# Keeping short-lived sums in PSUM, so that VectorE reads one operand there and one in SBUF

## The chip, the cores and the metric

One core of a Trainium2 chip runs the whole program. The metric is the device time of one execution in microseconds (us): 2315.3 us, the median of 3 runs before the change (2315.18 to 2316.68).

## The reference, cut to what matters

Two transformer blocks stand one behind the other, on 512 tokens of width 1024, all in float32. The first is conditioned on a vector `c`; the second has two mixers and 64 experts.

```python
mod = silu(c) @ w_mod + b_mod                      # 1024 -> 9 * 1024
sh1, sc1, ga1, sh2, sc2, ga2, sh3, sc3, ga3 = split(mod, 9)
h = rms_norm(x, g_ffn1) * (1 + sc1) + sh1
x = x + 0.5 * (1 + ga1) * ((silu(h @ w1_gate) * (h @ w1_up)) @ w1_down)    # width 2816
h = rms_norm(x, g_mix) * (1 + sc2) + sh2
x = x + (1 + ga2) * hybrid_mixer(h)
h = rms_norm(x, g_ffn2) * (1 + sc3) + sh3
x = x + 0.5 * (1 + ga3) * swiglu(h, w2_gate, w2_up, w2_down)
x = second_block(x)          # two mixers, then a router and 64 experts
```

## The kernel before

The activations are held transposed: eight tiles `xT` of 128 features by 512 tokens. Each float32 matrix product is made of three products of rounded parts: a weight panel is rounded by ScalarE (`wh`) and its rest is taken by GpSimd in pieces of 256 columns (`wl`, line 131); an activation is split into a high part by ScalarE and a low part by VectorE (`split`, lines 105 and 106). There are eight banks of PSUM, 128 by 512 float32 each: two under the name `mm` and six under `at`.

A feed-forward stage (`ffn_lined`) goes through 22 pairs of weight panels (gate and up, 128 hidden features each), in groups of 6, 6, 5 and 5. A pair costs TensorE 48 matmuls of 512 columns into two banks of `at`. Then ScalarE takes silu of the gate (line 538), VectorE multiplies by up (line 539), and the product is split into `ah` and `al` for the down product. Behind each group, `down` goes through the eight `xT` tiles: three matmuls for each pair of the group into a bank of `mm`, and VectorE adds the result to `xT` (line 551). The first down product of a group reads the group's pairs in order, so it needs the last pair's `ah` and `al` only near its end.

In the first feed-forward stage a callback, `between`, stands behind the pairs 2 to 15. Each call computes one of 14 half chunks of 512 columns of `mod`: two loads of 1 MB (`wmod`, four buffers), eight VectorE operations that add up 128x512 rows times a column of `silu(c)` (`modacc`, lines 276 and 278, two buffers in SBUF), and three bfloat16 parts of the sum (`third`, lines 285 to 291) made by ScalarE and GpSimd in turn. Twelve thin matmuls with a column of ones add over the partitions (`mod_cols`).

A norm (`norm_after`, `norm_half`) goes by halves of 256 tokens. As each `xT` tile gets its last update, ScalarE squares it and VectorE adds the square to a sum (line 338). A matmul with ones adds over the partitions, ScalarE makes 1/rms in two steps (`rstd`, lines 317 and 318), and for each of the eight tiles VectorE scales `xT` by it (line 351), ScalarE rounds, and VectorE takes the rest (`hl`, line 355 or 359). The first half's scaling is interleaved with the second half's updates. There are three such norms: behind the first feed-forward stage, behind the first mixer, and behind the second feed-forward stage.

A scheduler sets the order of the instructions on each engine when the program is built; it goes by the order of the source, by a price for each instruction, and by which buffers it expects to be free. Each engine then executes its own queue strictly in that order.

Of the kernel before, what the change touches and what calls it, by code (L numbers as in the profile page):

```python
# [7 lines left out]
F32 = mybir.dt.float32  # L8
# [9 lines left out]
P = 128  # L18
S = 512
D = 1024  # L20
KD = D // P
# [9 lines left out]
def f32(ap):  # L31
    return ap.bitcast(F32)


class Net:
# [225 lines left out]
    def mod_rows(self, pool, rs, on_pe=False):  # L261

        nc = self.nc
        acc = self.sb(pool, [P, 512], F32, "modacc", 2)
        if on_pe:

            pr = self.ps("mm")
            for kh in range(2):
                for k in range(4):
                    self.mm(pr[32 * k:32 * k + 32], self.cpad[:, kh * 4 + k], rs[kh][:, k], kh == 0, kh == 1)  # L270
            nc.vector.tensor_copy(acc, pr)
        else:
            for k in range(KD):
                c, r = self.ccol[:, k:k + 1], rs[k // 4][:, k % 4]
                if k == 0:
                    nc.vector.tensor_scalar(acc, r, c, None, op0=ALU.mult)
                else:
                    nc.vector.scalar_tensor_tensor(acc, r, c, acc, op0=ALU.mult, op1=ALU.add)  # L278
        return acc

    def thirds(self, pool, x):

        nc = self.nc
        parts = [self.sb(pool, [P, 512], BF16, f"third{i}", 2) for i in range(3)]
        nc.scalar.activation(parts[0], x, AF.Copy)
        halves = slice(0, 256), slice(256, 512)
        for cs in halves:
            nc.gpsimd.tensor_sub(x[:, cs], x[:, cs], parts[0][:, cs])  # L288
        nc.scalar.activation(parts[1], x, AF.Copy)
        for cs in halves:  # L290
            nc.gpsimd.tensor_sub(parts[2][:, cs], x[:, cs], parts[1][:, cs])  # L291
        return parts

    def mod_cols(self, chunk, half, parts):
# [34 lines left out]

    HALVES = (slice(0, 256), slice(256, 512))  # L330

    def square(self, j, half, acc):

        sq = self.tmp()[:, :256]
        self.nc.scalar.activation(sq, self.xT[j][:, self.HALVES[half]], AF.Square)
        if acc is None:
            return sq
        self.nc.vector.tensor_add(acc, acc, sq)  # L338
        return acc

    def norm_half(self, half, acc, acol, bcol, off, hs, between=lambda j: None):

        nc = self.nc
        pn = self.ps("at")[:, :256]
        self.mm(pn, self.ones, acc, True, True)
        r = self.rstd(pn, D, 256)
        ts = self.HALVES[half]
        cs = slice(off + ts.start, off + ts.stop)
        for j in range(KD):
            t = self.tmp()[:, :256]  # L350
            nc.vector.scalar_tensor_tensor(t, self.xT[j][:, ts], acol[:, j:j + 1], r, op0=ALU.mult, op1=ALU.mult)  # L351
            H, L = (t_[:, cs] for t_ in hs[j])
            if bcol is None:
                nc.scalar.activation(H, t, AF.Copy)
                nc.vector.tensor_sub(L, t, f32(H))
            else:
                b = bcol[:, j:j + 1]
                nc.scalar.activation(H, t, AF.Identity, bias=b)
                nc.vector.scalar_tensor_tensor(L, t, b, f32(H), op0=ALU.add, op1=ALU.subtract)  # L359
            between(j)  # L360

    def norm_after(self, steps, ahead, acol, bcol, off=0):


        acc = [None, None]
        self.pe_order_from = len(self.traced())
        if off:

            tags = [f"hl{j}" for j in range(4)] + [f"hh{j}" for j in range(4, KD)]
            tags += [f"h{part}{j}" for j in range(KD) for part in "hl" if f"h{part}{j}" not in tags]  # L370
            made = {tag: self.hidden2(F32R, tag) for tag in tags}
            hs = [(made[f"hh{j}"], made[f"hl{j}"]) for j in range(KD)]
        else:
            hs = [tuple(self.sb(self.hp, [P, S], F32R, f"h{part}{j}") for part in "hl") for j in range(KD)]

        def run(half, todo):
            for j, update in todo:
                update()
                acc[half] = self.square(j, half, acc[half])

        run(0, steps[0])
        run(1, steps[1][:ahead])
        rest = steps[1][ahead:]
        self.norm_half(0, acc[0], acol, bcol, off, hs, lambda j: rest and run(1, [rest.pop(0)]))
        return hs, lambda: self.norm_half(1, acc[1], acol, bcol, off, hs)
# [121 lines left out]
    def ffn_lined(self, pool, i, wg, wu, wd, nxt, hs, second, between):  # L507

        nc = self.nc
        groups = ((0, 6), (6, 12), (12, 17), (17, 22))  # L510
        if i == 0:
            hs, done = self.first_norm(pool, wg, wu)
        else:
            panels = [self.wpanel(w, f) for f in range(2) for w in (wg, wu)]
            done = [self.ps("at") for _ in panels]
            for half, ts in enumerate(self.HALVES):
                for n, (p, (wh, wl)) in enumerate(zip(done, panels)):
                    if half == 0 and n == 1:
                        second()
                    for k in range(KD):  # L520
                        self.mm3(p[:, ts], wh[:, k], wl[:, k], hs[k][0][:, ts], hs[k][1][:, ts], k == 0, k == KD - 1)
            self.pe_order()
        for f0, f1 in groups:
            act = []
            nf = f1 - f0
            for f in range(f0, f1):
                ps = []
                for w in (wg, wu):
                    if done:
                        ps.append(done.pop(0))  # L530
                        continue
                    wh, wl = self.wpanel(w, f)
                    p = self.ps("at")
                    for k in range(KD):
                        self.mm3(p, wh[:, k], wl[:, k], hs[k][0][:, :S], hs[k][1][:, :S], k == 0, k == KD - 1)
                    ps.append(p)
                s = self.sb(pool, [P, S], F32, "silu", 2)
                self.mark = nc.scalar.activation(s, ps[0], AF.Silu)
                nc.vector.tensor_mul(s, ps[1], s)  # L539
                ah = self.sb(pool, [P, S], F32R, "ah", 7)  # L540
                al = self.sb(pool, [P, S], F32R, "al", 7)
                self.split(ah, al, s)
                act.append((ah, al))
                between(f)

            def down(j, w, ts):
                p = self.ps("mm")[:, ts]
                for k in range(nf):
                    self.mm3(p, w[0][:, k], w[1][:, k], act[k][0][:, ts], act[k][1][:, ts], k == 0, k == nf - 1)
                x = self.xT[j][:, ts]  # L550
                nc.vector.scalar_tensor_tensor(x, p, self.G[i][:, j:j + 1], x, op0=ALU.mult, op1=ALU.add)

            def load(j):
                return self.kpanel(wd[f0 * P:f1 * P, j * P:(j + 1) * P], nf, P)

            if f1 < NF:
                for j in range(KD):
                    down(j, load(j), slice(0, S))
        self.use_exp()

        held = {}

        def step(j, half):
            if j not in held:
                held[j] = load(j)
            down(j, held[j], self.HALVES[half])
            if not half and j < 4:
                del held[j]

        return self.norm_after([[(j, lambda j=j: step(j, 0)) for j in range(KD)],  # L570
                                [(j, lambda j=j: step(j, 1)) for j in (4, 5, 6, 7, 0, 1, 2, 3)]], 1, *nxt)
# [1548 lines left out]
```

## Time and profile before

| | |
|---|---|
| median of 3 runs | 2315.3 us |
| the profiled execution: time, span of its core | 2318.89 us, 2317.1 us |
| first feed-forward stage with its start | about 0 to 406 us |
| first mixer, second feed-forward stage | to about 753 us, to about 1090 us |
| second block's mixers, then router and experts | to about 1350 us, to the end |
| busy: PE, DVE, ACT, POOL | 91%, 35%, 26%, 34% of the span |

PE is TensorE, DVE VectorE, ACT ScalarE, POOL GpSimd. The profile is of one execution. A line such as L89 is the line of the kernel that issues an instruction; L89 is the one place for all matmuls, so these are told apart by their tiles. The durations of PE are modelled and overlap: the distance between the starts of two matmuls is the pace, 0.23 us for 512 columns in the full stretches.

### The profile page before, as it was taken

What the parts mean: (1) busy time and instruction counts of PE and PEld (TensorE: products, weight loads), DVE (VectorE), ACT (ScalarE), POOL (GpSimd) and SP (SyncE); (2) the same over time, 40 slices, a digit from 0 to 9 for tenths busy, and PEclk for the clock granted to TensorE, in tenths of its full rate; (3) what the DMA queues carried; (4) which work ended last, traced back from release to release, by engine and by line L of the source; (5) the groups of instructions that cost most, each with busy time, mean ns of one, the idle gap of its engine ahead of it and who ended that gap; (6) DMA issues with size and microseconds to landing.
All of it is one profiled execution on the core that took longest, in us unless ns stands there. A gap on an engine that the chain in (4) does not pass through costs nothing.

```text
span 2317.1 us, 29183 instructions
## 1 busy us (share of the span) xinstructions
PE 2103.3 (91%) x11561; PEld 1390.1 (60%) x11561; DVE 814.6 (35%) x1390; ACT 595.8 (26%) x1027; POOL 791.2 (34%) x1023
## 2 busy tenths in 40 slices
PE   8889999999998999999999999988888598888886
PEld 5767788887877888888887763332333243333332
DVE  6748321657578211112635552111111111111112
ACT  4323222465365322223524421000000000000002
POOL 2869655775543455555655300000000000000001
PEclk9999999999999999999999999999999799999997
DMA  9676322421211232333422199999999999999998
GB/s 328 222 245 218 101 86 86 110 75 38 73 46 47 80 102 83 107 101 87 107 69 83 58 378 415 421 421 421 421 421 420 378 421 420 420 421 420 421 421 302
DMA packets 275921, 550.10 MB, mean 237 GB/s; under 512 B 18461, under 2 KB 199862, under 8 KB 228678
## 3 DMA queue, kind: packets, MB, share of 16 engines
q1 hardware_dynamic: 272832, 547.78, 62.9%
q8 instruction: 92, 1.51, 0.3%
q10 hardware_dynamic: 2950, 0.43, 0.1%
q14 instruction: 47, 0.39, 0.0%
HBM read 546.06 MB, written 2.10 MB: 237 GB/s over the span
## 4 chain that ended last, share of the span: by engine, by line
PE 50%; DMA 36%; DVE 8%; POOL 3%; ACT 2%; issue 1%; SPq 0%; POOLq 0%; ACTq 0%; DVEq 0%
PE at L89 32%; PE mm L89 17%; DMA ew<-in_expert_w_gate 12%; DMA ew<-in_expert_w_down 12%; DMA ew<-in_expert_w_up 11%; POOL wl L131 2%; DVE modacc L278 1%; DMA wmod<-in_w_mod 1%; DVE tmp L351 1%; DVE tmp L338 1%; DVE hl L359 1%; POOL modacc L288 0%; POOL third L291 0%; DVE smax L866 0%; PE at L1351 0%
## 5 line engine op out<-in xcount | busy, mean ns | idle before, releaser
L131 POOL TENSOR_TENSOR wl<-wraw,wh 128x256 fp32r<-128x256 f32 (+1 forms) x790 | 613.4, 807 | 403.2 <-ACT wh L123 401.3
L89 PE MATMUL at<-ew,xg 128*32 128x512 f32 x2048 | 330.8, 647 | 71.4 <-DMA ew<-in_expert_w_up 44.4
L1814 POOL TENSOR_TENSOR sg<-oh,Gt 128x512 f32<-128x512 f32 x16 | 16.8, 1050 | 852.6 <-PE at L1866 565.5
L89 PE MATMUL at<-hh,wh 128*128 128x512 f32 (+3 forms) x800 | 298.7, 377 | 3.1 <-ACT hh L450 1.2
L123 ACT ACTIVATE wh<-wraw 128x1024 fp32r<-128x1024 f32 (+2 forms) x193 | 183.9, 954 | 454.0 <-PE at L89 187.0
L89 PE MATMUL at<-hl,wh 128*128 128x512 f32 (+3 forms) x800 | 296.5, 375 | 3.7 <-DVE hl L359 1.5
L89 PE MATMUL at<-hh,wl 128*128 128x512 f32 (+3 forms) x800 | 294.8, 373 | 0.0
L89 PEld LDWEIGHTS at<-ew,xg 128*32 128x32 f32 x2048 | 75.4, 116 | 283.9 <-issue 142.0
L89 PE MATMUL at<-ew,ehT 128*32 128x512 f32 (+1 forms) x1040 | 186.5, 599 | 18.9 <-ACT ehT L1878 10.4
L89 PE MATMUL mm<-ah,wh 128*128 128x512 f32 (+1 forms) x432 | 155.8, 361 | 22.5 <-ACT ah L105 12.8
L89 PEld LDWEIGHTS at<-hh,wh 128*128 128x128 f32 (+1 forms) x800 | 150.4, 188 | 33.3 <-ACT hh L450 3.5
L89 PEld LDWEIGHTS at<-hl,wh 128*128 128x128 f32 (+1 forms) x800 | 150.7, 188 | 32.3 <-DVE hl L359 2.4
L89 PEld LDWEIGHTS at<-oh,xn 128*128 128x128 f32 x1024 | 123.2, 197 | 73.1 <-issue 70.8
L89 PEld LDWEIGHTS at<-hh,wl 128*128 128x128 f32 (+1 forms) x800 | 150.7, 189 | 26.2
L89 PE MATMUL mm<-al,wh 128*128 128x512 f32 (+1 forms) x432 | 154.1, 357 | 2.9 <-DVE al L106 2.9
L89 PE MATMUL at<-oh,xn 128*128 128x128 f32 x1024 | 135.2, 287 | 20.8 <-DMA ew<-in_expert_w_gate 19.5
L89 PE MATMUL mm<-ah,wl 128*128 128x512 f32 (+1 forms) x432 | 153.5, 355 | 0.0
L1901 DVE TENSOR_TENSOR ewa<-ewa,mm 128x512 f32<-128x512 f32 (+1 forms) x124 | 82.9, 670 | 167.8 <-PE mm L89 167.8
L539 DVE TENSOR_TENSOR silu<-at,silu 128x512 f32<-128x512 f32 x44 | 30.3, 689 | 286.8 <-PE at L89 279.0
L1873 DVE SCALAR_TENSOR_TENSOR eh<-at,rslot,eh 128x512 f32<-128x512 f32 x16 | 17.3, 1084 | 323.4 <-PE at L89 323.4
L89 PE MATMUL mm<-ey,sgT 128*128 128x512 f32 (+1 forms) x264 | 125.0, 604 | 2.0 <-DVE ewa L1904 0.8
L89 PEld LDWEIGHTS at<-ew,ehT 128*32 128x32 f32 x1040 | 46.6, 111 | 126.4 <-issue 81.4
(483 smaller groups left out, 3118.8 us busy)
## 6 DMA issues: line engine op xcount, KB each, us to landing
ew<-in_expert_w_gate SPq DMA_DIRECT2D x128, 1024.0 KB, 19.8
ew<-in_expert_w_up SPq DMA_DIRECT2D x128, 1024.0 KB, 19.8
ew<-in_expert_w_down SPq DMA_DIRECT2D x122, 1024.0 KB, 19.8
wmod<-in_w_mod SPq DMA_DIRECT2D x36, 1024.0 KB, 8.4
wraw<-in_w_gate SPq DMA_DIRECT2D x44, 512.0 KB, 3.9
wraw<-in_w_up SPq DMA_DIRECT2D x44, 512.0 KB, 3.8
wraw<-in_w_in SPq DMA_DIRECT2D x39, 512.0 KB, 3.9
wraw<-in_w_down SPq DMA_DIRECT2D x40, 320.0 KB, 3.2
```

The source lines that it names most:

```text
L89: self.nc.tensor.matmul(out, lhsT, rhs, start=start, stop=stop, skip_group_check=open_)
L123: self.nc.scalar.activation(h[:, :cols], r[:, :cols], AF.Copy)
L131: (eng or self.nc.gpsimd).tensor_sub(l[:, cs], r[:, cs], f32(h[:, cs]))
L278: nc.vector.scalar_tensor_tensor(acc, r, c, acc, op0=ALU.mult, op1=ALU.add)
L338: self.nc.vector.tensor_add(acc, acc, sq)
L351: nc.vector.scalar_tensor_tensor(t, self.xT[j][:, ts], acol[:, j:j + 1], r, op0=ALU.mult, op1=ALU.mult)
L359: nc.vector.scalar_tensor_tensor(L, t, b, f32(H), op0=ALU.add, op1=ALU.subtract)
L539: nc.vector.tensor_mul(s, ps[1], s)
L1814: nc.gpsimd.tensor_tensor(sg.rearrange("p t (e s) -> p t e s", s=self.CAP), ov, self.G[:, :, es_].unsqueeze(3).to_broadcast(shp), op=ALU.mult)
L1873: nc.vector.scalar_tensor_tensor(hf, pu, rs, hf, op0=ALU.mult, op1=ALU.mult)
L1901: nc.vector.tensor_add(self.acc[t][:, cs], self.acc[t][:, cs], pc[:, :w])
```

## The change

Four kinds of values that lay in SBUF now lie in PSUM, in banks of `at`:

- The modulation's sum (`modacc`), from its first operation to the second subtraction. [...]
- The product of silu and up: VectorE writes it over up. `split` then reads it from there, and the bank is held until `al` is made.
- The sums of squares: the second addition writes into a bank, the later ones add there, and the last writes to SBUF again, since TensorE reads it.
- 1/rms: ScalarE writes it over the sum that it comes from.

```diff
     def mod_rows(self, pool, rs, on_pe=False):
-        acc = self.sb(pool, [P, 512], F32, "modacc", 2)
         if on_pe:
+            acc = self.sb(pool, [P, 512], F32, "modacc", 2)
...
         else:
+            acc = self.ps("at")
             for k in range(KD):
...
         nc.scalar.activation(parts[0], x, AF.Copy)
-        halves = slice(0, 256), slice(256, 512)
-        for cs in halves:
-            nc.gpsimd.tensor_sub(x[:, cs], x[:, cs], parts[0][:, cs])
+        nc.vector.tensor_sub(x, x, parts[0])
         nc.scalar.activation(parts[1], x, AF.Copy)
-        for cs in halves:
-            nc.gpsimd.tensor_sub(parts[2][:, cs], x[:, cs], parts[1][:, cs])
+        nc.vector.tensor_sub(parts[2], x, parts[1])
         return parts
...
-    def square(self, j, half, acc):
+    def square(self, n, j, half, acc):
         sq = self.tmp()[:, :256]
         self.nc.scalar.activation(sq, self.xT[j][:, self.HALVES[half]], AF.Square)
-        if acc is None:
+        if n == 0:
             return sq
-        self.nc.vector.tensor_add(acc, acc, sq)
-        return acc
+        to = self.ps("at")[:, :256] if n == 1 else acc if n < KD - 1 else self.tmp()[:, :256]
+        self.nc.vector.tensor_add(to, acc, sq)
+        return to
...
         pn = self.ps("at")[:, :256]
         self.mm(pn, self.ones, acc, True, True)
-        r = self.rstd(pn, D, 256)
+        r = self.rstd(pn, D, 256, r=pn)
...
                 self.mark = nc.scalar.activation(s, ps[0], AF.Silu)
-                nc.vector.tensor_mul(s, ps[1], s)
+                nc.vector.tensor_mul(ps[1], ps[1], s)
+                s = ps[1]
                 ah = self.sb(pool, [P, S], F32R, "ah", 7)
                 al = self.sb(pool, [P, S], F32R, "al", 7)
                 self.split(ah, al, s)
```

The scheduler orders the program anew. VectorE at the end of the first group of the first feed-forward stage, before: `silu_974` is the product of pair 5, the last of the group, `al_978` its low part, and `modacc_1432` the modulation's sum of pair 7.

```order
L276 TENSOR_SCALAR modacc_1432<-wmod_1428,ccol_153 128x512
L278 SCALAR_TENSOR_TENSOR modacc_1432<-wmod_1428,ccol_153,modacc_1432 128x512 x3
L278 SCALAR_TENSOR_TENSOR modacc_1432<-wmod_1430,ccol_153,modacc_1432 128x512 x3
L539 TENSOR_TENSOR silu_974<-at_949,silu_974 128x512
L304 TENSOR_TENSOR mod_61<-mm_1003,cols_68 128x4
L278 SCALAR_TENSOR_TENSOR modacc_1432<-wmod_1430,ccol_153,modacc_1432 128x512
L106 TENSOR_TENSOR al_978<-silu_974,ah_977 128x512
L309 SCALAR_TENSOR_TENSOR A_3_63<-mod_61,cols_68 128x4
```

The same place now: `at_943` is up and then the product of pair 5, and `at_979` the modulation's sum of pair 5 itself.

```order
L278 TENSOR_SCALAR at_979<-wmod_975,ccol_153 128x512
L280 SCALAR_TENSOR_TENSOR at_979<-wmod_975,ccol_153,at_979 128x512 x3
L280 SCALAR_TENSOR_TENSOR at_979<-wmod_977,ccol_153,at_979 128x512 x3
L541 TENSOR_TENSOR at_943<-at_943,silu_968 128x512
L280 SCALAR_TENSOR_TENSOR at_979<-wmod_977,ccol_153,at_979 128x512
L106 TENSOR_TENSOR al_972<-at_943,ah_971 128x512
L288 TENSOR_TENSOR at_979<-at_979,third_208_988 128x512
L290 TENSOR_TENSOR third_210_990<-at_979,third_209_989 128x512
L303 TENSOR_TENSOR mod_61<-mm_995,cols_68 128x4
L308 SCALAR_TENSOR_TENSOR A_3_63<-mod_61,cols_68 128x4
```

Before, the sums ran up to two pairs ahead of the pair whose product is made between them. Now each pair's product and sum stand together, and the sum of the next pair begins only behind the small operations that close this one (lines 303 and 308).

TensorE at the border of the pairs 2 and 3, before: the last matmuls of pair 2 (`at_613`), then the thin matmuls of its half chunk (`third_154` to `third_156`), twelve in one piece, and behind them pair 3.

```order
L89 MATMUL at_613<-hl_131_492,wh_606 128x512
L89 MATMUL at_613<-hh_130_490,wl_608 128x512
L89 LDWEIGHTS third_154_658
L89 MATMUL mm_667<-onesb_139,third_154_658 128x1
L89 LDWEIGHTS third_155_659
L89 MATMUL mm_667<-onesb_139,third_155_659 128x1
L89 LDWEIGHTS third_156_660
L89 MATMUL mm_667<-onesb_139,third_156_660 128x1
```

The same thin matmuls now, within pair 3's gate (`at_689`).

```order
L89 MATMUL at_689<-hh_98_337,wh_682 128x512
L89 LDWEIGHTS third_154_658
L89 MATMUL mm_665<-onesb_139,third_154_658 128x1
L89 MATMUL at_689<-hl_99_339,wh_682 128x512
L89 MATMUL at_689<-hh_98_337,wl_684 128x512
L89 MATMUL at_689<-hh_124_478,wh_682 128x512
L89 MATMUL at_689<-hl_125_480,wh_682 128x512
L89 MATMUL at_689<-hh_124_478,wl_684 128x512
L89 MATMUL at_689<-hh_126_482,wh_682 128x512
L89 LDWEIGHTS third_155_659
L89 MATMUL mm_665<-onesb_139,third_155_659 128x1
```

The first thin matmul moved behind 10 matmuls of the next gate, the second behind 16, and the remaining ten behind 20.

## Rows read from the trace of the kernel before

**Rows 1.** The page, the chain that ended last, shares of the span by engine.

```profile
PE 50%; DMA 36%; DVE 8%; POOL 3%; ACT 2%; issue 1%; SPq 0%; POOLq 0%; ACTq 0%; DVEq 0%
```

**Rows 2.** PE in order of time: start, us, instruction, [idle before <- releaser].

```profile
103.77 0.45 PE L89 MATMUL mm<-onesb,third 128*128 128x1 bf16 x12
107.90 0.50 PE L89 MATMUL mm<-ah,wh 128*128 128x512 f32 x1 [3.68 <-DVE mod L304]
119.53 0.80 PE L89 MATMUL mm<-ah,wh 128*128 128x512 f32 x1 [6.32 <-ACT ah L105]
```

**Rows 3.** DVE in order of time, the same stretch.

```profile
103.49 0.98 DVE L276 TENSOR_SCALAR modacc<-wmod,ccol 128x512 f32<-128x512 f32 x1 [6.18 <-POOL wl L131]
...
118.14 0.68 DVE L539 TENSOR_TENSOR silu<-at,silu 128x512 f32<-128x512 f32 x1
```

**Rows 4.** A stretch: length, busy PE, PEld, DVE, ACT, POOL, PEclk, DMA share, GB/s.

```profile
120.00:125.00 5.00, 4.22 (x10) 3.12 (x10) 1.66 (x2) 1.99 (x3) 4.26 (x7) 0.50 0.82 272
```

**Rows 5.** The chain in order of time, 140 to 350 us: start, us, what.

```profile
156.28 10.88 PE at L89 x48
...
266.02 10.88 PE at L89 x48
276.90 0.29 PE mm L89 x12
277.20 11.02 PE at L89 x48
...
322.16 27.26 PE mm L89 x120
```

**Rows 6.** PE in order of time, the second group's down product.

```profile
223.89 0.47 PE L89 MATMUL mm<-ah,wh 128*128 128x512 f32 x1
...
234.05 0.80 PE L89 MATMUL mm<-ah,wh 128*128 128x512 f32 x1 [6.48 <-ACT ah L105]
```

**Rows 7.** DVE groups by shape, whole span: count | busy us, mean ns | idle before.

```profile
L278 DVE SCALAR_TENSOR_TENSOR modacc<-wmod,ccol,modacc 128x512 f32<-128x512 f32 x98 | 100.2, 1023 | 3.0
...
L551 DVE SCALAR_TENSOR_TENSOR xT<-mm,G,xT 128x512 f32<-128x512 f32 x48 | 36.0, 750 | 116.3 <-PE mm L89 116.3
L539 DVE TENSOR_TENSOR silu<-at,silu 128x512 f32<-128x512 f32 x44 | 30.3, 689 | 286.8 <-PE at L89 279.0 <-ACT silu L538 7.8
```

**Rows 8.** DVE groups, 49 to 53.5 us (POOL idle), then 187 to 208 us.

```profile
L278 DVE SCALAR_TENSOR_TENSOR modacc<-wmod,ccol,modacc 128x512 f32<-128x512 f32 x6 | 4.5, 752 | 0.2
...
L278 DVE SCALAR_TENSOR_TENSOR modacc<-wmod,ccol,modacc 128x512 f32<-128x512 f32 x14 | 15.5, 1109 | 0.5
```

**Rows 9.** POOL groups, 145 to 160 us, then 187 to 208 us.

```profile
L131 POOL TENSOR_TENSOR wl<-wraw,wh 128x256 fp32r<-128x256 f32 x16 | 11.3, 738 | 5.6 <-ACT wh L123 5.6
...
L131 POOL TENSOR_TENSOR wl<-wraw,wh 128x256 fp32r<-128x256 f32 x16 | 17.0, 1095 | 0.0
```

**Rows 10.** ACT groups by shape, whole span.

```profile
L285 ACT ACTIVATE third<-modacc 128x512 bf16<-128x512 f32 x14 | 8.7, 621 | 19.3 <-DVE modacc L278 19.3
```

**Rows 11.** Stretches of the three norms.

```profile
425.00:460.00 35.00, 30.84 (x230) 29.30 (x230) 29.42 (x50) 17.34 (x36) 29.70 (x40) 0.95 0.45 121
735.00:760.00 25.00, 19.86 (x127) 17.85 (x127) 20.77 (x38) 13.62 (x28) 13.42 (x16) 0.86 0.29 85
1110.00:1130.00 20.00, 15.82 (x110) 14.33 (x108) 17.60 (x32) 9.57 (x18) 19.08 (x31) 0.91 0.67 175
```

**Rows 12.** DVE in order of time, one tile's turn in the first norm.

```profile
432.07 1.00 DVE L351 SCALAR_TENSOR_TENSOR tmp<-xT,A,tmp 128x256 f32<-128x256 f32 x1
432.99 0.96 DVE L338 TENSOR_TENSOR tmp<-tmp,tmp 128x256 f32<-128x256 f32 x1
433.87 0.47 DVE L551 SCALAR_TENSOR_TENSOR xT<-mm,G,xT 128x256 f32<-128x256 f32 x1
434.27 0.56 DVE L359 SCALAR_TENSOR_TENSOR hl<-tmp,mod,hh 128x256 fp32r<-128x256 f32 x1
```

**Rows 13.** The chain in order of time, where the norm begins.

```profile
406.52 14.90 PE mm L89 x122
```

More of the change, by code (lines that the diff above doesn't have):

```diff
@@ L362, in norm_after @@
     def norm_after(self, steps, ahead, acol, bcol, off=0):
-        acc = [None, None]
+        acc, n = [None, None], [0, 0]
         self.pe_order_from = len(self.traced())
@@ L378, in run @@
                 update()
-                acc[half] = self.square(j, half, acc[half])
+                acc[half] = self.square(n[half], j, half, acc[half])
+                n[half] += 1
         run(0, steps[0])
```

## The prediction

> **What bounds the kernel now.** I read the chain that ended last first. PE holds half of it and DMA 36% [rows 1]; the DMA share is the experts' weights in the last 970 us, which the change does not touch. So the question is where TensorE waits before that, and for whom. I then read the stretches one after the other for PE's idle time and its granted clock, and PE in order of time where it was idle. Two places stand out: the ends of the first two groups of the first feed-forward stage, and the three norms.
>
> First group: PE ends pair 5 with the thin matmuls at 103.77 + 0.45, about 104.1, and starts the down product at 107.90, after 3.68 us of waiting; it waits 6.32 us more before 119.53 [rows 2]. The second wait is for `ah` of the last pair, whose product VectorE made only at 118.14, 14 us after PE had finished the pair [rows 3]. VectorE was late because the modulation's operations stand ahead of the product in its queue, and at 103.49 it had itself waited 6.18 us for GpSimd to free a `modacc` buffer [rows 3]. [...] Second group: PE starts the down product at 223.89 and waits 6.48 us before 234.05, again for `ah` [rows 6].
>
> What these two cost, waits and slow clock together: the third group's down product, undisturbed, takes 27.26 us for 120 matmuls, 0.227 us each [rows 5], so 144 take 32.7 us. The first took from 104.1 to 156.28, 52.2 us: 19.5 lost. The second took from 223.89 to 266.02, 42.1 us: 9.4 lost [rows 2, 5, 6]. Together 28.9 us.
>
> Why VectorE and GpSimd are slow there: an addition to `modacc`, two operands from SBUF, takes 752 ns while GpSimd is idle and 1109 ns while it works; GpSimd's `wl` takes 738 ns where VectorE is nearly idle and 1095 ns beside those additions [rows 8, 9]. The update of `xT`, the same operation with one operand from PSUM, takes 750 ns in the mean of 48 [rows 7].
>
> **The change part by part.** *The modulation.* 98 additions at 1023 ns [rows 7] become additions with one operand in PSUM. No row shows VectorE writing PSUM. Bounds: 750 ns, the row that reads PSUM and has the same three inputs [rows 7], and 1109 ns, the worst of today [rows 8]; a gain below 0.75 is bounded by the 0.69 of a plain product [rows 7]. I take 0.75, since the write is the only thing that differs from that row. 56 GpSimd operations become 28 on VectorE, 0.69 each, and GpSimd's `wl` falls towards 738 ns.
>
> The order matters more than the durations. The sum of a pair now begins when the previous pair is closed, so VectorE's round, from one product to the next, must fit into PE's 11.02 + 0.29 = 11.3 us a pair [rows 5]. The round is a chain: product 0.69, `ah` 0.62, first third 0.62, subtraction 0.69, second third 0.62, subtraction 0.69 [rows 7, 10], ten of the twelve thin matmuls, at most 0.45 [rows 2]; this is 4.4. For the small 128x4 operations and the handovers I allow 1 us, an estimate. Then the first operation of the next sum, 0.69, and six additions at 0.77 with their gaps, 4.6. Total 10.7 us, 0.6 below PE's pace. `modacc` no longer waits for GpSimd.
>
> The thin matmuls now stand inside the next gate, behind 10, 16 and 20 matmuls, so 2.3, 3.6 and 4.5 us after the pair's end at 0.227 each. By the chain the thirds are ready at about 1.9 + 0.3, 3.3 + 0.4 and 4.0 + 0.5 us, the added part being handovers and one weight copy that stands ahead of `ah` in ScalarE's queue. PE, which executes in order, then waits some 0.3 us a pair, and the rest of the gate is queued behind: 14 x 0.3 = 4 us. At the two group ends the second down product needs the bank of `mm` that the thin matmuls hold until line 303, about 1 us each: 2. The last pair's `ah` and `al` are needed 15 matmuls, 3.4 us, into the down product and are there after about 2.2. So of 28.9 us 23 come back. Bounds: 15, if PE waits 0.7 us a pair and 2 us at each group end, and 29.
>
> [...]
>
> *The product of silu and up* already reads PSUM, 689 ns [rows 7], and only its output moves. `al` then reads PSUM as well and is no longer held up; outside the group ends PE does not wait for it, so I count nothing. The bank of up is held until `al`, about 1.5 us longer. At most four or five of the six banks are then in use (two of a pair, one sum, two of the next), so nothing is late by that.
>
> *The norms.* A turn of VectorE in the first norm is four operations, from 432.07 to 434.83, overlapping a little: 2.7 us [rows 12]. PE's part of a turn is 15 matmuls at 14.90 / 122 = 0.122: 1.83 us [rows 13]. So VectorE sets the pace there, and PE idles. With 1/rms and the sum in PSUM, the scaling (1.00) and the addition (0.96) should come down to the 0.47 of the `xT` update beside them [rows 12], which has an operand in PSUM. `hl` keeps two operands in SBUF: 0.56 to 0.96. The turn is then 1.7 to 2.1 us with the same overlap, near PE's. Over the three norms PE was idle for 35 - 30.84, 25 - 19.86 and 20 - 15.82, 13.5 us in all, and the clock of 0.95, 0.86 and 0.91 on the busy rest costs 1.5 + 2.8 + 1.4 = 5.7 [rows 11]. VectorE's excess over PE falls from 0.85 to between 0 and 0.25 a turn, so 70% or more of these 19.2 us should go, but the first and last tile of a half still wait for the chain norm, scale, round, rest. I take 13, bounds 7 and 17. ScalarE's writing of 1/rms in place is six pairs of small steps: nothing.
>
> *Sum.* 23 + 13 = 36 us. Everything behind shifts as it is: the mixers are bound by PE, the experts' loads start when buffers of the earlier stages come free. The profiled execution took 2318.9 us, 1.8 more than its span and 3.6 more than the median. 2318.9 - 36 = 2282.9, less 3.6: **2279 us**.
>
> **The rivals.** *One: the operations stay slow.* If VectorE's second operand still waits for GpSimd, or if reading and writing the same bank holds it up, an addition costs about 1.02. The round holds nine operations that write PSUM, one after the other (product, subtraction, seven of the next sum): 9 x 0.27 = 2.4 us more, 1.8 beyond the slack, 25 us over 14 pairs. The first stage gains nothing and half of the norms is left: about 2308. For it: no row has such an output. Against: the 48 updates of `xT` read PSUM beside a busy GpSimd at 750 [rows 7].
>
> *Two: slower.* If an operation on one bank in place needed its reading and its writing one after the other, 1.5 us, the round would be 9 x 0.75 - 0.6 = 6.2 us over PE's pace; 14 x 6.2 = 86 us lost, against 29 gained there, and the norms' two operations at 0.94 are where they were: about 2370. It decides from an in-place operation of about 1.05 in the first stage alone, and 1.15 with the norms' gain. For it, only that nothing shows the contrary.
>
> *Three: given back.* Sums no longer run ahead, so a late load shows at once. A pair needs 2 MB of `w_mod` and 1 MB of panels in 11.3 us, some 280 GB/s with the MB taken as 2^20 bytes; the engines moved 272 GB/s at a share of 0.82 [rows 4], which leaves a fifth. If the queue's order makes each load 2 us late, 14 x 2 = 28 us go and the gain is the norms' and little else: about 2307 to 2311.
>
> **How the numbers follow.** The forecast's own case, 25 to 48 us faster, has 0.76; rival one 0.10; rival three 0.07, of which a part lies within 0.2%; rival two 0.07. A measurement of this kernel tells a change from none at about 0.2%, 4.6 us. Faster by more: 0.76 + 0.09 + 0.04 = 0.89; the same 0.04; slower 0.07. The range: the low end lies 8 us beyond the upper bounds of 29 + 17 = 46 us, for waits that I took as fixed, 2261; the high end takes in part of rivals one and three, 2302.
>
> **What would show it.** Right: additions to the sum (line 280) near 0.75 us and `wl` near 0.74 at 180 to 220 us; the two down products at about 33 to 35 us each; waits of PE for `third` of tenths of a us a pair; a norm's turn at 2 us. Wrong: additions above 1 us; PE's pairs at 12 us or more with waits for `third` in each; loads of `wmod` that VectorE waits for; norms in which PE idles as before, now for `hl` or for ScalarE.

## The result and the profile after

The changed kernel takes 2283.66 us (median of 4 runs, 2278.09 to 2286.39); the kernel before took 2315.99 us beside it. The ratio is 0.985, interval 0.983 to 0.9869: 1.5% faster, 32 us by the medians and some 35 by the ratio. Forecast were 2279 us and a range of 2261 to 2302.

The profiled execution of the change has a span of 2276.4 us, 40.7 less than that of before. Marks that stand in both chains (the start of the fourth group's gate and later blocks of the same length) divide this sum:

| stretch | before, us | after, us | gain |
|---|---|---|---|
| start to the fourth group's gate | 349.42 | 331.21 | 18.2 |
| from there over the first norm into the first mixer | 132.54 | 126.26 | 6.3 |
| the first mixer | 243.72 | 244.73 | -1.0 |
| second norm | 94.54 | 88.67 | 5.9 |
| second feed-forward stage | 212.26 | 212.16 | 0.1 |
| third norm, into the second mixers | 192.51 | 188.72 | 3.8 |
| the rest | 1092.1 | 1084.65 | 7.4 |

The rest is chance, not the change. Before, PE waited there 4.18 us for an update of `xT`, which stood in VectorE's queue behind an operation that took 6.23 us; in the first trace of the change that operation took 0.72 us and PE did not wait, and in a second trace of the same changed kernel (span 2281.1 us) it did (the last section shows the operation). PE in order of time, second trace:

```profile
1224.53 0.77 PE L89 MATMUL at<-qh,wh 128*128 128x512 f32 x1 [4.17 <-DVE xT L1027]
```

There the rest took 1090.85 us. Without the rest the traces of before and after differ by 33 us, which is what the timed runs say.

The chain that ended last, shares of the span by engine, against [rows 1]: VectorE (from 8% to 5%) and GpSimd (from 3% to 1%) have given way to PE.

```profile
PE 56%; DMA 35%; DVE 5%; ACT 2%; issue 1%; POOL 1%; SPq 0%; ACTq 0%; POOLq 0%; DVEq 0%
```

VectorE's groups by shape over the whole span, against [rows 7]:

```profile
L280 DVE SCALAR_TENSOR_TENSOR at<-wmod,ccol,at 128x512 f32<-128x512 f32 x98 | 73.9, 754 | 3.0
L541 DVE TENSOR_TENSOR at<-at,silu 128x512 f32<-128x512 f32 x44 | 30.8, 699 | 271.5 <-PE at L89 260.7 <-ACT silu L539 10.7
L106 DVE TENSOR_TENSOR al<-at,ah 128x512 fp32r<-128x512 f32 x44 | 30.4, 691 | 21.7 <-ACT ah L105 21.1
L359 DVE SCALAR_TENSOR_TENSOR hl<-tmp,mod,hh 128x256 fp32r<-128x256 f32 x32 | 20.2, 656 | 1.4 <-ACT hh L358 1.4
...
L351 DVE SCALAR_TENSOR_TENSOR tmp<-xT,A,at 128x256 f32<-128x256 f32 x32 | 14.2, 472 | 3.5 <-ACT at L317 3.5
L338 DVE TENSOR_TENSOR at<-at,tmp 128x256 f32<-128x256 f32 x30 | 12.8, 428 | 8.5 <-ACT tmp L334 8.2
...
L278 DVE TENSOR_SCALAR at<-wmod,ccol 128x512 f32<-128x512 f32 x14 | 10.4, 746 | 0.0
```

The additions cost 745 to 757 ns in all 98 cases, 754 in the mean, whatever GpSimd does; before it was 752 to 1109 [rows 8]. In the norm `hl` and the first addition of two squares (line 338, 924 ns, 6 of them), the operations with two operands in SBUF that are left there, are still slow.

The end of the first group, PE in order of time, against [rows 2]: the waits of 3.68 and 6.32 us have become one of 2.21, but a slow stretch still follows, with a granted clock of 0.50 as in [rows 4]. At the second group's end the wait of 6.48 us [rows 6] has become one of 2.21 too, before 213.14; behind that one the granted clock stays at 1.00 (211 to 216 us).

```profile
104.37 0.39 PE L89 MATMUL at<-hh,wl 128*128 128x512 f32 x1
106.96 0.19 PE L89 MATMUL mm<-onesb,third 128*128 128x1 bf16 x1 [2.21 <-ACT third L287]
107.01 0.77 PE L89 MATMUL mm<-ah,wh 128*128 128x512 f32 x1
```

Stretches, with the columns of [rows 4]: behind that wait, then the three norms, each begun about as far behind the start of its norm as in [rows 11].

```profile
107.00:110.00 3.00, 3.00 (x9) 2.09 (x10) 1.33 (x2) 0.60 (x1) 0.72 (x2) 0.50 0.55 175
406.00:441.00 35.00, 34.05 (x278) 33.35 (x277) 25.42 (x52) 18.00 (x39) 33.25 (x47) 1.00 0.50 136
711.00:736.00 25.00, 22.64 (x175) 21.35 (x174) 19.94 (x46) 14.95 (x31) 12.55 (x16) 1.00 0.29 86
1080.00:1100.00 20.00, 18.43 (x135) 17.28 (x134) 15.33 (x38) 11.56 (x24) 17.71 (x31) 0.91 0.68 179
```

PE is idle for 0.95, 2.36 and 1.57 us there in place of 4.16, 5.14 and 4.18.

The chain in order of time over two pairs and to the fourth gate, against [rows 5]: a pair now falls into pieces, with a start every 11.65 us (192.79 - 181.14) where it was 11.31.

```profile
181.14 8.75 PE at L89 x38
190.01 1.48 PE at L89 x6
192.79 8.75 PE at L89 x38
...
213.14 33.48 PE mm L89 x156
...
331.21 54.41 PE at L89 x240
```

### The profile page after: what moved, and what is told of

Read it like the earlier page. It is cut to its first block, busy times and chain, and to the rows that moved or that the text cites. A ratio compares the mean times of both kernels' runs of the same rounds, so it can differ in the third digit from the quotient of the medians.

```text
span 2276.4 us, 29153 instructions
## 1 busy us (share of the span) xinstructions
PE 2094.8 (92%) x11561; PEld 1379.9 (61%) x11561; DVE 775.6 (34%) x1418; ACT 594.6 (26%) x1027; POOL 700.5 (31%) x967
## 4 chain that ended last, share of the span: by engine, by line
PE 56%; DMA 35%; DVE 5%; ACT 2%; issue 1%; POOL 1%; SPq 0%; ACTq 0%; POOLq 0%; DVEq 0%
PE at L89 38%; PE mm L89 18%; DMA ew<-in_expert_w_up 12%; DMA ew<-in_expert_w_gate 11%; DMA ew<-in_expert_w_down 11%; DMA wmod<-in_w_mod 1%; DVE hl L359 1%; DMA wraw<-in_w_in 0%; POOL wl L131 0%; DVE smax L869 0%; PE at L1354 0%; ACT pc L877 0%; DVE tmp L351 0%; DVE pc L882 0%; DVE pb L106 0%
## 5 line engine op out<-in xcount | busy, mean ns | idle before, releaser
L131 POOL TENSOR_TENSOR wl<-wraw,wh 128x256 fp32r<-128x256 f32 (+1 forms) x790 | 564.2, 745 | 484.3 <-ACT wh L123 482.3
L89 PE MATMUL at<-oh,xn 128*128 128x128 f32 x1024 | 135.0, 287 | 20.8 <-issue 19.5
L541 DVE TENSOR_TENSOR at<-at,silu 128x512 f32<-128x512 f32 x44 | 30.8, 699 | 271.5 <-PE at L89 260.7
```

Source lines behind the costliest of these rows:

```text
L89: self.nc.tensor.matmul(out, lhsT, rhs, start=start, stop=stop, skip_group_check=open_)
L131: (eng or self.nc.gpsimd).tensor_sub(l[:, cs], r[:, cs], f32(h[:, cs]))
L541: nc.vector.tensor_mul(ps[1], ps[1], s)
```

## The experiments

Twelve runs in three sets of four, each set timed beside the kernel before (medians there 2316.26, 2317.45 and 2311.43 us); ratios are to the kernel before of the same set. The first set took the change apart.

**The modulation alone** (lines 261 to 291 of the change, the rest as before).

> Only the modulation's part of the change: the sum in PSUM, the thirds' subtractions on VectorE; the norms and the product of silu and up as before. My theory: the first feed-forward stage gains what it gained in the full change, 18 to 20 us (the third group's down product starts at 304 us in place of 322), the norms stay as before; about 2297 us. Additions at 0.75 us. Rival (the parts help only together, the stage needs the product and al in PSUM too): VectorE's al stays near 0.96 us and the gain is under 10 us, above 2305.

Measured: ratio 0.9916 (0.9899 to 0.9932), 2295.4 us; the fourth gate starts at 330.08 us, additions at 755 ns, `al` still 934. My theory holds, the rival falls: `al` at its old price costs this stage nothing.

**The norms alone.**

> Only the norms' part: sums of squares and 1/rms in PSUM; modulation and product as before. My theory: the first feed-forward stage is as before, the three norms give 14 us (5.8 + 3.9 + 4.5), 2301 us. Rival (the norms get faster in the full change because GpSimd or the DMA queue come into them at another time): under 5 us, 2311 or more.

Measured: 0.994 (0.9925 to 0.9956), 2301.8 us. The fourth gate is at 349.29, as before; the three stretches of the table with a norm give 5.8, 5.9 and 3.8 us. Holds.

**The subtractions moved to VectorE, the sum left in SBUF.** The edit, on the kernel before:

```
-        for cs in halves:
-            nc.gpsimd.tensor_sub(x[:, cs], x[:, cs], parts[0][:, cs])
+        nc.vector.tensor_sub(x, x, parts[0])
...
-            nc.gpsimd.tensor_sub(parts[2][:, cs], x[:, cs], parts[1][:, cs])
+        nc.vector.tensor_sub(parts[2], x, parts[1])
```

> The kernel before with one edit: the 56 subtractions of 256 columns move from GpSimd to VectorE as 28 of 512 columns; the sum stays in SBUF, as do norms and product. My theory (the place of the operand decides, not GpSimd's release): additions stay near 1.0 us beside GpSimd's wl, the subtractions take about 1.1 us each, VectorE's round of a pair grows from some 9.8 to 12 us and more, beyond PE's 11.3, and the stage does not gain: between 0 and 20 us slower, 2315 to 2335. Rival (the stage gained because GpSimd was relieved and no longer holds the sum's buffers): 15 to 20 us faster, 2296 to 2300.

Measured: 0.9914 (0.9896 to 0.9931), 2296.85 us: as much as the modulation's whole part, with no sum in PSUM. My theory falls. VectorE's and GpSimd's groups, 45 to 300 us, of this kernel:

```profile
L278 DVE SCALAR_TENSOR_TENSOR modacc<-wmod,ccol,modacc 128x512 f32<-128x512 f32 x98 | 94.3, 962 | 4.0 <-DMA wmod<-in_w_mod 1.2
L106 DVE TENSOR_TENSOR al<-silu,ah 128x512 fp32r<-128x512 f32 x16 | 16.7, 1043 | 0.6 <-ACT ah L105 0.4
L288 DVE TENSOR_TENSOR third<-modacc,third 128x512 bf16<-128x512 f32 x14 | 15.3, 1093 | 1.2 <-ACT third L287 1.2
```

```profile
L131 POOL TENSOR_TENSOR wl<-wraw,wh 128x256 fp32r<-128x256 f32 x172 | 157.9, 950 | 102.3 <-ACT wh L123 102.3
```

The operations are about as slow as I had said, and the stage is faster all the same. By these means a pair's work on VectorE is 7 x 0.96 + 0.62 + 0.69 + 1.04 + 0.78 + 1.09 = 10.9 us, where I had put it at 12. In the second group the round from one product to the next (line 536 here, 539 before) is longer than that, 11.4 to 11.8 us and 10.6 for the last, about PE's 11.31; it was 12.0 to 12.9 before, so that VectorE falls behind far less. VectorE in order of time, here and then before:

```profile
196.03 0.69 DVE L536 TENSOR_TENSOR silu<-at,silu 128x512 f32<-128x512 f32 x1
...
207.82 0.68 DVE L536 TENSOR_TENSOR silu<-at,silu 128x512 f32<-128x512 f32 x1
```

```profile
208.55 0.68 DVE L539 TENSOR_TENSOR silu<-at,silu 128x512 f32<-128x512 f32 x1
...
220.66 0.68 DVE L539 TENSOR_TENSOR silu<-at,silu 128x512 f32<-128x512 f32 x1
```

What went is the waiting for GpSimd: VectorE's idle time before the first operation of a sum (21.9 us before, of which 14.6 ended with GpSimd) is 1.7. In these two rounds the seven additions also fell from 7.9 to 7.0 us. The profiled execution was 9 us slower than the median; in it the fourth gate starts at 334.65, so by the trace 14.8 us came in this stage. PE in order of time shows one large wait, at the end of the first group, and none at the second:

```profile
116.92 0.80 PE L89 MATMUL mm<-ah,wh 128*128 128x512 f32 x1 [9.28 <-ACT ah L105]
```

**The sum in PSUM, the subtractions left on GpSimd**, from a copy that ScalarE makes in SBUF:

```
+        y = self.sb(pool, [P, 512], F32, "modacc", 2)
+        nc.scalar.activation(y, x, AF.Copy)
...
+            nc.gpsimd.tensor_sub(y[:, cs], y[:, cs], parts[0][:, cs])
```

> The modulation's sum in PSUM, but the subtractions stay on GpSimd: ScalarE copies the sum to SBUF first (one more 128x512 copy, 0.6 us a chunk), then as before. My theory: additions at 0.75 us; GpSimd's subtractions come back (28 x 2 of about 0.7 to 0.8 us, 3 us a pair) behind wl in its queue, so the thirds are late for the place at which PE has them, and PE waits for them in each pair, 1 to 2 us: part of the 19 us is lost, 2298 to 2320. Rival (only the sum's bank matters): as the modulation's part alone, 2297.

Measured: 1.013 (1.0111 to 1.0148), 2345.97 us. The direction of my theory, but far more: 30 us slower than before. PE in order of time, one pair:

```profile
217.58 0.18 PE L89 MATMUL mm<-onesb,third 128*128 128x1 bf16 x1 [1.95 <-ACT third L293]
...
219.83 0.63 PE L89 MATMUL at<-hh,wh 128*128 128x512 f32 x1
...
224.86 0.40 PE L89 MATMUL at<-hh,wh 128*128 128x512 f32 x1
```

The second third is late by 1.95 us here, and by 0.7 to 2.1 us once a pair in 13 of the 14. After it the matmuls start every 0.43 us and not 0.227, until 224.5. The stretch around it, 17 us for one pair, has a granted clock of 0.80:

```profile
214.00:231.00 17.00, 14.87 (x61) 11.18 (x60) 7.92 (x12) 4.48 (x7) 8.08 (x13) 0.80 0.52 169
```

The first thirds of two pairs stand at 214.19 and 231.25, 17.06 us apart, where a pair of the change, with its thin matmuls in three places as well, takes 11.65: the wait of 2 us costs 17.06 - 11.65 = 5.4. That is what the change would have cost had it moved the sum and not the subtractions (the extra copy included): by these runs the sum's move pays only with the subtractions moved, and not the other way round.

The second set took the rest apart and tried a better order.

**The changed kernel again.**

> The changed kernel once more, for a second trace of it. My theory: of the 40.7 us between the two profiled spans, 5.9 us (PE's wait for xT and the rope tables at 1255 us of the trace before) and about 1.8 us at the end are chance of that execution; the first stage ends again near 388 us and the three norms take the same; the span lies between 2276 and 2285. Rival: the 5.9 us belong to the change, and the wait is never there in it.

Measured: 0.9854 (0.9839 to 0.9869), 2283.47 us, span 2281.1; the fourth gate at 329.96, the three norm stretches 126.3, 88.1 and 188.8. The wait of 4.17 us is back (shown above), so it belongs to the execution and the rival falls.

**The thin matmuls together and late:**

```
-            for i, part in enumerate(parts):
+            for i, part in enumerate(reversed(parts)):
...
-                        n.mod_cols(c, h, n.thirds(p, n.mod_rows(p, n.load_mod(p, c, h))))
+                        parts = n.thirds(p, n.mod_rows(p, n.load_mod(p, c, h)))
+                        if last:
+                            return lambda: n.mod_cols(c, h, parts, "at")
+                        n.mod_cols(c, h, parts)
...
                     down(j, load(j), slice(0, S))
+                    if j == 0 and late:
+                        late()
```

> The changed kernel, with the twelve thin matmuls of a chunk together in one place, behind 20 matmuls of the next gate (the parts are added in the order third, second, first), and at the first two group ends behind 20 matmuls of the first down product, their sums in a bank of at. My theory: a pair's pace falls from 11.65 us to 11.35, since two of three switches to the thin matmuls go (about 0.1 us each) and the wait for the first third (0.1): 11 x 0.3 = 3.3 us; the two waits of 2.2 us and the slow clock behind the first (1.5 us) go: 5.9 us. Together 7 to 9 us faster than the change, 2273 to 2276. Rival (the pair's pace is VectorE's round): pairs stay at 11.65 and only the group ends gain, 5 us or less.

Measured: 0.9805 (0.9791 to 0.9818), 2272.45 us: 11 us faster than the change beside it, some more than the 7 to 9. PE waits for no third at all. The chain in order of time:

```profile
103.03 4.53 PE mm L89 x20
107.86 28.25 PE mm L89 x124
...
151.81 11.02 PE at L89 x48
163.12 11.02 PE at L89 x48
...
319.95 54.41 PE at L89 x240
```

A pair takes 163.12 - 151.81 = 11.31 us again, and a group's down product 136.10 - 103.03 = 33.1 us, next to the 32.7 of 144 undisturbed matmuls. The rival (VectorE's round sets the pair's pace) falls.

**The product of silu and up alone.**

> Only the product of silu and up in PSUM, from where al reads it. My theory: al falls from 0.96 to 0.69 us; nothing waits for it but at the ends of the two feed-forward stages: 1 to 3 us faster, 2312 to 2315. Rival (VectorE's queue in the first stage is what makes the last pair's product late, so 0.27 us a pair adds up to the group's end): 4 to 6 us faster.

Measured: 0.9984 (0.9973 to 0.9995), 2315.5 us beside 2317.45; `al` at 692 ns, the fourth gate 0.9 us earlier. As my theory.

**1/rms alone.**

> Only 1/rms written in place in PSUM; the sums of squares stay in SBUF. My theory: a tile's turn of VectorE in the first half of a norm loses only the 0.2 to 0.5 us of the scaling, the addition of 0.66 to 0.96 us stays, and half of the norms' 14 us come: 5 to 9 us, 2306 to 2310. Rival (the chain scale, round, rest sets the turn, not VectorE's sum): all of the 14 us, 2301.

Measured: 0.9938 (0.9925 to 0.9952), 2304.07 us. By time this is as much as the norms' whole part, as the rival has it. By the trace's stretches it is 6.3, 1.0 and 2.5 us, 9.8 in all against 15.5, as my theory has it: the scaling at 468 ns, the addition of squares still at 616. The times can't tell the two apart, so how much the sums of squares add stays open.

The third set asked what the sum's place in PSUM is worth.

**The change with the sum in SBUF:**

```
-            acc = self.ps("at")
+            acc = self.sb(pool, [P, 512], F32, "modacc", 2)
```

> The full change, but with the modulation's sum in SBUF (two buffers, as before); the subtractions on VectorE, norms and product as in the change. Theory formed after the subtractions alone, with the sum in SBUF, had given as much time as the modulation's whole part: what the first stage gained is GpSimd's release, and the sum's place adds at most the 4.6 us that the two traces differ by at the fourth group's gate (334.65 against 330.08 us): 2283 to 2288, the fourth gate at 331 to 335 us. Rival (the sum in PSUM carries the stage): the gate at 340 or later, 2292 or more.

Measured: 0.9854 (0.9838 to 0.9869), 2278.95 us: the same ratio as the change, 0.985 and 0.9854. The fourth gate is at 331.66, 0.5 and 1.7 us later than in the two traces of the change. The new theory holds. PE in order of time, then the chain, show where the same sum comes from:

```profile
115.31 0.80 PE L89 MATMUL mm<-ah,wh 128*128 128x512 f32 x1 [8.18 <-ACT ah L105]
```

```profile
215.25 33.08 PE mm L89 x156
248.33 10.88 PE at L89 x48
259.50 11.02 PE at L89 x48
```

With the sum in SBUF the sums run ahead, the thin matmuls stand behind the pair, a pair takes 11.31 us and the second group's end is without loss; but the first group's end waits 8.18 us. VectorE in order of time shows for what: operations of the next sum and its thirds stand ahead of the product (line 541), for which PE's pair had been ready at 103.3.

```profile
107.50 2.34 DVE L280 SCALAR_TENSOR_TENSOR modacc<-wmod,ccol,modacc 128x512 f32<-128x512 f32 x2
109.77 1.20 DVE L290 TENSOR_TENSOR third<-modacc,third 128x512 bf16<-128x512 f32 x1
110.89 3.12 DVE L280 SCALAR_TENSOR_TENSOR modacc<-wmod,ccol,modacc 128x512 f32<-128x512 f32 x3
113.94 0.69 DVE L541 TENSOR_TENSOR at<-at,silu 128x512 f32<-128x512 f32 x1
```

**The better order with the sum in SBUF.**

> As the kernel with the thin matmuls together and late, but with the modulation's sum in SBUF. Theory: with the sum in SBUF its additions stand ahead of the last pair's product in VectorE's queue, so the group ends still wait for ah, and the later place of the thin matmuls gives little: 2279 to 2286, the fourth gate near 330 us. So in the better order the sum in PSUM is worth 8 to 12 us. Rival (the order alone did it): as with the sum in PSUM, 2271 to 2275, the gate at 320 to 322 us.

Measured: 0.9855 (0.9839 to 0.9872), 2278.28 us; the gate at 332.56, the wait for `ah` 8.20 us. As the theory: the later thin matmuls are worth nothing here.

**The scaled tile in PSUM too:**

```
-            t = self.tmp()[:, :256]
+            t = self.tmp()[:, :256] if half else self.ps("at")[:, :256]
```

> As the kernel with the thin matmuls together and late; in addition the scaled tile of the first half of each norm (line 351) is written to a bank of at, so that hl (line 359) has one operand in PSUM. Theory: hl falls from 0.66 to about 0.5 us there, a tile's turn by 0.1 to 0.2 us, in three norms of 8 tiles: 1 to 4 us faster than without it, about 2270. Rival (the banks of at run out, and the scaling waits for one): no gain or up to 5 us slower, 2273 to 2278.

**The better order once more.**

> The kernel with the thin matmuls together and late once more, beside the two built on it: 2272, the fourth gate at 320 us. What its several timings differ by between calls is the scale on which the two are judged.

Measured: 0.9799 (0.9781 to 0.9817) with the scaled tile, 0.9798 (0.9785 to 0.9812) without: no difference. `hl` did fall, to 474 ns. The second and third norm are 1.5 to 2.5 us shorter each, but the first is 3.6 longer, by an accident told in the last section, not by the banks as the rival had it. The better order itself repeats its gain, at 2266.6 us beside 2311.43, and no kernel here is faster; its gate is at 322.06 since that execution's start took 2 us longer.

## Why the prediction was right, and where its reason was not

*Operations.* The addition was taken at 0.75 us, bounds 0.69 to 1.109: 754 ns, and the rivals with an in-place operation of 1.02 or 1.5 us fall with it. `al`, the scaling and the sums of squares came down as the neighbours had shown (691, 472 and 428 ns). One price was mis-sized: the first operation of a sum, taken at 0.69, is 746 ns with its output in PSUM; with it in SBUF, before, it took 477 at the least and 820 in the mean. An addition with the sum in PSUM took 745 to 757 ns, one with both operands in SBUF at the least 735 (the subtractions moved, the sum left in SBUF).

*The first stage, 23 us expected (15 to 29).* Up to the fourth gate 18.2 and 19.5 us came, in two traces. Of the terms, the pairs' 0.3 us is right (0.29 to 0.34, in 12 pairs), but not as a wait: each third had its own place between the thick matmuls, and a change to thin matmuls and back costs about 0.12 us (around the second third 0.58 us, 191.11 to 191.69, in place of two matmuls at 0.227); the wait for the first third is 0.1. The 1 us at each group end was too small: 2.2 us, and 1.4 more at the first, where seven matmuls ran at half pace (a start every 0.43 us, 107.59 to 109.72); with the thin matmuls' places 2.6 and 4.1. I had looked at when the bank comes free and not at where the first thin matmul stands: here no gate stands ahead of it, it stands ahead of the whole down product, and so PE waits out all of the 2.2 us that the prediction itself has up to the first third. In ScalarE's queue, behind PE's last matmul at 104.37, stand a weight copy (to 105.54), `ah` (to 106.20) and only then that third (to 106.91). 28.9 - 3.7 - 4.1 - 2.6 = 18.5, next to what came.

*VectorE's round, 10.7 us.* Right, 10.9 (11.65 less the wait shown here): VectorE in order of time waits for PE before a pair's product,

```profile
187.74 0.70 DVE L541 TENSOR_TENSOR at<-at,silu 128x512 f32<-128x512 f32 x1 [0.78 <-PE at L89]
```

so that PE and not VectorE sets the pace, and the better order's 11.31 us shows it.

*The norms, 13 us (7 to 17).* The stretches give 16.0 and 16.4 us, in the second trace as in the first. A turn is 2.0 us, as VectorE in order of time shows against [rows 12]:

```profile
409.94 0.47 DVE L351 SCALAR_TENSOR_TENSOR tmp<-xT,A,at 128x256 f32<-128x256 f32 x1
410.34 0.42 DVE L338 TENSOR_TENSOR at<-at,tmp 128x256 f32<-128x256 f32 x1
410.67 0.47 DVE L554 SCALAR_TENSOR_TENSOR xT<-mm,G,xT 128x256 f32<-128x256 f32 x1
411.06 0.96 DVE L359 SCALAR_TENSOR_TENSOR hl<-tmp,mod,hh 128x256 fp32r<-128x256 f32 x1
```

*The sum, 36 us.* Part of its closeness is luck: the first stage gave 3.5 to 4.8 us less than expected and the norms 3.0 to 3.4 more.

*The step that failed is a reason, not a number.* I let the first stage's gain hang on the operand's rate in PSUM: rival one had it that additions at 1.02 us gain nothing there. The runs showed additions at 0.96 us, in SBUF, with the same gain by time. (Rival one's own case, slow additions in a sum that is tied to its pair, no run made.) What brought the gain is that the subtractions left GpSimd, whose `wl` they had stood behind, so that VectorE no longer waited for a buffer of the sum. The sum's place in PSUM exchanges one loss for others: it ties each sum to its pair, which removes the last wait of 8.2 us and the slow clock behind it (with the sum in SBUF, a matmul every 0.43 us from 116.63), and pays some 0.3 us a pair (12 times, 3.7 us) and 4.1 + 2.6 us at the two group ends. With the thin matmuls placed for it, those costs are gone and the place is worth 12 us after all (0.9798 against 0.9855 for the same order with the sum in SBUF, 2266.6 and 2278.28 us in one set).

*Given back, rival three.* No load of `wmod` is late in the stage after its start: in the trace of the change VectorE waits for none before the 112 operations of the sums (lines 278 and 280). The rival falls.

## What to carry to other kernels

When an operation moves both to another memory and to another engine, run each half alone: for the modulation's sum here the engine made the whole difference in time, the memory none until the thin matmuls were placed for it, and moving only the memory (with ScalarE's copy of the sum to SBUF) was 30 us slower. By the fourth gate the engine alone made 14.8 us, and 17.8 with norms and product in PSUM, of 18.2 to 19.5. When a change ties two streams together that ran apart, look at where the follow-up work lands in the engine that executes in order: gather it in one place that is late enough for all of it. Count a wait of PE by what the clock does after it, here 5.4 us for one of 1.95, where one of 2.21 at the second group's end had no slow clock behind it.

## What the hardware showed unexpectedly

A VectorE operation of four columns took 5.48 us. In the kernel with the scaled tile in PSUM the preparation of a 128x4 constant of the mixer, both sides in SBUF, came while GpSimd was at a row of `wl`. VectorE in order of time, then GpSimd:

```profile
406.50 5.48 DVE L893 TENSOR_SCALAR gq<-cols 128x4 f32<-128x4 f32 x1
```

```profile
403.34 8.33 POOL L131 TENSOR_TENSOR wl<-wraw,wh 128x256 fp32r<-128x256 f32 x12
```

It ended some 0.3 us after GpSimd's twelve operations (403.34 + 8.33 = 411.67). In six other traces (before, the norms alone, both of the change, both of the better order) it took 0.65 to 0.70 us. PE then waited 3.62 us for `hl`, which stood behind it, with a granted clock of 0.83 over 410 to 420 us. By the times here the operation on VectorE lasted over seven or eight operations of GpSimd's row (5.48 us, at 8.33 / 12 = 0.69 each). What decides it stays open: in the first trace of the change GpSimd was in such a row as well, and the operation took 0.65 us.

The wait of 4.2 us in the rest of the program goes back, by the times again, to the same thing. `ql`, a low part of 128x512 in the second block, is taken by VectorE from two operands in SBUF (line 106), twice, while GpSimd begins a row of eight. In six traces (before, the second of the change, the product alone, 1/rms alone, the first of the better order, the scaled tile) the two took 6.8 us together. In that of before the first took 6.23 us and ended 0.55 us after GpSimd's row, whose operations took 0.71 to 0.73 us each. In two traces (the first of the change, the norms alone) the two took 1.9 us together; in that of the change the first took 0.72 us, and GpSimd's slowest operation in the row 1.19. VectorE and GpSimd in the second trace of the change, then in the first:

```profile
1216.95 6.83 DVE L106 TENSOR_TENSOR ql<-tmp,qh 128x512 fp32r<-128x512 f32 x2
...
1217.11 5.52 POOL L131 TENSOR_TENSOR wl<-wraw,wh 128x256 fp32r<-128x256 f32 x8
```

```profile
1218.46 1.87 DVE L106 TENSOR_TENSOR ql<-tmp,qh 128x512 fp32r<-128x512 f32 x2
...
1218.60 6.86 POOL L131 TENSOR_TENSOR wl<-wraw,wh 128x256 fp32r<-128x256 f32 x8
```

The rope tables that the expectation of the second trace names were not what was late: in the trace before, the chain has the last of them landed at 1255.10 us, and VectorE was in `ql`, which does not read them, until 1257.94. Whether moving the constant away from the norm would give the 1.5 to 2.5 us of the other norms was not tried.
